# The first mixer's modulation pieces on TensorE: four strips of 32 columns in place of a share between TensorE and VectorE, and no subtractions on GpSimd in that phase

## The chip, the cores and the metric

The kernel runs on one core of one Trainium2 chip. The metric is the device time of one execution in microseconds (us); for a kernel it is the median of its runs. The core's engines have queues of their own and wait for each other by semaphores: TensorE (PE; its weight loads are listed apart as PEld), VectorE (DVE), ScalarE (ACT), GpSimd (POOL), and SyncE (SP), which here only starts DMA transfers. Each queue is worked off in its own fixed order.

## The reference, cut to what matters

Two layers of a trunk, on 256 tokens of 1024 numbers, everything in float32. A condition vector `c` steers each layer through six modulation vectors of 1024 numbers:

```python
c_act = jax.nn.silu(c)
for l in range(DEPTH):
    mod = c_act @ w_ada[l] + b_ada[l]
    sh_m, sc_m, g_m, sh_f, sc_f, g_f = [m[:, None, :] for m in jnp.split(mod, 6, -1)]
    h = rms_norm(x, norm_mix[l]) * (1.0 + sc_m) + sh_m
    proj = h @ w_in[l]
    ...
    y = (gate_a * y_a + gate_b * y_b) @ w_out[l]
    x = x + g_m * y
    h = rms_norm(x, norm_ffn[l]) * (1.0 + sc_f) + sh_f
    ...
    x = x + g_f * f
```

So nothing of the first projection `h @ w_in[0]` can be multiplied before the shift `sh_m` and the scale `sc_m` of layer 0 are known. They are 2048 of the 6144 columns of `c_act @ w_ada[0]`, a product of one row of 1024 numbers with a matrix of 8 MB. The layers' mixers (a gated delta rule and a sparse attention) and feed-forward parts (dense in layer 0, eight experts in layer 1) follow.

## The kernel before, in words

**Layout.** Activations lie transposed: 128 features on the partitions, 8 tiles of features (`k` = 0 to 7), 256 tokens along a row. A modulation vector must therefore end as columns, feature on partition; they stand in `modc`. The weights come from memory in pieces of 1 MB (512 columns by 4 feature tiles), one after the other on SP's queue, into slots that are used again when their readers are done.

**A modulation piece, `ada` (L248) and `flush` (L264).** A piece is 512 columns of `w_ada`, two transfers of four feature tiles each. Multiplying by `c_act` and adding over features is done in two ways. TensorE's part (L256): `cact[:, k]`, one column, is the stationary operand, and the 512 columns stream past it into row 0 of the bank `pada`. VectorE's part (L258, L260): each of the 128 partitions multiplies its 512 numbers by its own `cact` and adds them into `acc`, so the sum over partitions is still open. `NPE` says how many of the eight tiles TensorE takes: 4, 4, 0 and 2 for the pieces at columns 0, 1024, 512 and 1536. `flush` adds TensorE's row to row 0 of `acc` (L271), closes the sum over partitions and turns it into columns by four matmuls with a column of ones (L283), and adds the bias into `modc` (L285). `flush` of a piece is called after the next piece's products.

**The input of the mixer, `norm_mod` (L316 on).** For each feature tile VectorE scales `xT` into `hm0f` (L340), ScalarE adds the shift and rounds to float32r, giving `hm0h` (L341), and VectorE forms the rest that the rounding lost, `hm0l` (L344). It runs in two halves of four tiles: `part=0` needs the pieces 0 (shift) and 1024 (scale), `part=1` the pieces 512 and 1536.

**The weights of the projection, `split` (L218 on).** Each weight block is split in the same way: ScalarE rounds it (`wh`, `wnh`, L233), another engine subtracts to get the rest (`wl`, `wnl`, L235). Each product is then three matmuls: rounded by rounded, and the two cross terms (L239 to L241 in `chunk_b`, L370 to L372 in `chunk_t`). Which engine subtracts is `cur["lo"]`; in the phase in question it is set to GpSimd, later to VectorE.

**The phase.** TensorE transposes `x` (L125); pieces 0 and 1024; half 0 of the input; then the first halves of three projection blocks, begun while half 1 of the input is not there yet: 264 columns of `b` (`pn`), 512 columns of `k` and, after the pieces 512 and 1536, 512 columns of `q` (`pj`). Then half 1 of the input, and everything that needs all eight tiles. Beside this GpSimd computes angles for the position tables (`tables`, L390 on), which end in a sine on ScalarE (L417).

**Order.** Up to `manual.close()` PE, DVE and SP do their work in the order in which the code is written; ACT's and POOL's order is set by the scheduler's own model of times. After that the scheduler orders all engines but SP until the experts.

Of the kernel before, what the change touches and what calls it, by code (L numbers as in the profile page):

```python
# [9 lines left out]
F32 = mybir.dt.float32  # L10
F32R = mybir.dt.float32r
I32 = mybir.dt.int32
AF = mybir.ActivationFunctionType
OP = mybir.AluOpType
AX = mybir.AxisListType

P = 128
D = 1024
KT = 8
# [2 lines left out]
SPLM = 1  # L22
RAWM = 2
QTAG = (("pj", "dn", "ns"), ("dn", "ns", "pj"))
NPE = (4, 4, 0, 2)
S = 256
NT = 2
PIN = 5416
# [58 lines left out]
def trunk(ctx, tc, A, out, dbg=None, stop=None):  # L87
# [11 lines left out]
    cur = {}  # L99

    def bank(tag, name="ps"):
        if tag == "mi":
            seq["mi"] = seq.get("mi", -1) + 1
            tag = ("no", "pj", "pj")[seq["mi"] % 3]
        return cur["psum"].tile([P, 512], F32, tag=tag, name=name, bufs=cur["bufs"][tag])
# [8 lines left out]
    mm = nc.tensor.matmul  # L114
    V, SC, G = nc.vector, nc.scalar, nc.gpsimd
# [37 lines left out]
    ini = es0.enter_context(tc.tile_pool(name="init", bufs=1))  # L153
# [20 lines left out]
    cact = cst.tile([P, 8], F32, name="cact")  # L174
# [2 lines left out]
    V.tensor_scalar(cact, cact, 1.0, None, op0=OP.add)  # L177
    V.reciprocal(cact, cact)
    V.tensor_tensor(cact, cact, pt[:, 0:8], op=OP.mult)
    b_ada = cols[:, 0, 0:96]  # L180
    n_mix = cols[:, 0, 96:112]
    n_ffn = cols[:, 0, 112:128]
# [5 lines left out]
    acc = act.tile([P, NT, D], F32, tag="acc", name="acc")  # L188
# [14 lines left out]
    def load(src, k, n, name, per=0):  # L203

        per = per or min(k, 2048 // n // 4 * 4)
        rs = []
        for k0 in range(0, k, per):
            r = slot_raw(name)
            m = min(per, k - k0)
            r = r[:, :m * n].rearrange("p (k n) -> p k n", k=m)  # L210
            nc.sync.dma_start(r, src[:, k0:k0 + m])
            rs.append(r)
        return lambda k_, n_=None: rs[k_ // per][:, k_ % per] if n_ is None else rs[k_ // per][:, k_ % per:k_ % per + n_]
# [31 lines left out]

    pend = []

    def ada(l, o, tag="pj", npe=0, turn=False):  # L248


        w = load(A["w_ada"][l][:, o:o + 512].rearrange("(k p) n -> p k n", p=P), KT, 512, f"ada{l}_{o}")
        acc = cur["tmp"].tile([P, 512], F32, tag="adacc", name=f"adacc{l}_{o}", bufs=2)
        pa = bank(tag, "pada") if npe else None
        for k in range(KT):
            if k % 4 < npe // 2:
                mm(pa[0:1], cact[:, k:k + 1], w(k), start=k == 0, stop=k == KT - 5 + npe // 2)  # L256
            elif k == npe // 2:
                V.tensor_scalar(acc, w(k), cact[:, k:k + 1], None, op0=OP.mult)  # L258
            else:
                V.scalar_tensor_tensor(acc, w(k), cact[:, k:k + 1], acc, op0=OP.mult, op1=OP.add)  # L260
        flush()
        pend.append((l, o, acc, tag, pa, turn))

    def flush():  # L264
        if not pend:
            return
        l, o, acc, tag, pa, turn = pend.pop()
        if pa is None:
            pa = bank(tag, "pada")
        else:  # L270
            V.tensor_tensor(acc[0:1], acc[0:1], pa[0:1], op=OP.add)  # L271
        if turn:

            red = cst.tile([P, 16], F32, tag="red", name="red", bufs=2)
            for i in range(2):
                tt = cur["tmp"].tile([P, S], F32, tag="ht", name="adat", bufs=3)
                V.transpose(tt, acc[:, i * S:i * S + S])
                V.tensor_reduce(red[:, i * 8:i * 8 + 8], tt.rearrange("p (b r) -> p b r", r=32), axis=AX.X, op=OP.add)
            for q in range(4):
                mm(pa[q * 32:q * 32 + 32, 0:4], C["mod32"], red[:, q::4], start=True, stop=True)  # L280
        else:
            for j in range(4):
                mm(pa[:, j:j + 1], acc[:, j * P:(j + 1) * P], ones[:, 0:1], start=True, stop=True)  # L283
        j0 = o // P
        V.tensor_tensor(modc[l][:, j0:j0 + 4], pa[:, 0:4], b_ada[:, l * 48 + j0:l * 48 + j0 + 4], op=OP.add)  # L285
# [25 lines left out]
    def norm_scale(sums, name):  # L311

        return rsq(sums[:, 0:NT], 2, 1.0 / D, name + "r", None)
# [1197 lines left out]
    for t in range(NT):  # L1511
        for q in range(2):
            px = bank("dn", "px")
            for j in range(4):
                k = q * 4 + j
# [2 lines left out]
    ss = cst.tile([P, NT], F32, name="ss")  # L1518
    for t in range(NT):
        SC.activation(cur["tmp"].tile([P, D], F32, tag="sqx", name="sqx"), xtok[:, t], AF.Square, accum_out=ss[:, t:t + 1])  # L1520
    ada(0, 0, npe=NPE[0])
    rx = norm_scale(ss, "hm0")
    columns(0, r1)
    V.tensor_scalar(cols[:, 0, 96:128], cols[:, 0, 96:128], 1.5, None, op0=OP.mult)
    ada(0, 1024, npe=NPE[1])
    pb = norm_bc(rx)
    pbs = ini.tile([P, S], F32, name="pbs")
    SC.activation(pbs, pb[:, 0:S], AF.Copy)
# [4 lines left out]
    raw_k = win_half(0, 512, 512)  # L1533
    raw_q = win_half(0, 0, 512)
    hx = norm_mod(0, 0, "hm0", pbs, part=0)
    cur["lo"] = G
    begun[O_B] = [bank("ns", "pn") for _ in range(NT)]
    chunk_t(begun[O_B], raw_b, hx, 264, (0,))
    begun[512] = [chunk_b(raw_k, hx, j * P, tag="pj", ks=(0,)) for j in (0, 2)]
    ada(0, 512, "no", npe=NPE[2])  # L1540
    small(0)
    ada(0, 1536, "dn", npe=NPE[3])
    begun[0] = [chunk_b(raw_q, hx, j * P, tag="dn", ks=(0,)) for j in (0, 2)]
    small(1)
    tables()
# [70 lines left out]
```

## Time and profile before

| what | value |
|---|---|
| time, median of 3 runs | 1790.15 us (1789.74 to 1791.38) |
| profiled execution | 1790.63 us, of it span of the trace 1788.8 us |
| PE busy | 1715.6 us, 96% of the span |
| DVE busy | 1263.3 us, 71% |
| ACT busy | 934.4 us, 52% |
| POOL busy | 61.7 us, 3% |
| read from memory | 512.13 MB |

A row of the timeline gives the start and the length in us, the engine, the line in the kernel, the operation with the tile that it writes and those that it reads, its shape, and the number of instructions that were merged into it; in brackets stands how long the engine was idle before it and what ended that. A float32 matmul leaves two records on PE, so the four products of a piece are "x8". A "busy" time can hold stalls inside an instruction: the same shape on the same engine with a longer time is a sign of it.

### The profile page before, as it was taken

The page shows a single profiled execution, that of the slowest core. Times are in us where ns is not written, and L with a number is a line of the kernel's source. Part 1 is how long each engine was busy: PE and PEld are TensorE (multiplying, and loading weights), DVE is VectorE, ACT ScalarE, POOL GpSimd, SP SyncE. Part 2 cuts the span into 40 slices and gives each one's busy share as a digit, 9 for nine tenths or more (in the row PEclk, how much of TensorE's full clock was granted, in tenths as well). Part 3 has the DMA queues.
Part 4 walks back from the last instruction along what each step waited for, and adds up shares of the span by engine and source line. Part 5 has one row for each costly group of instructions (what it writes and reads, how often), then busy time and mean ns, then how long its engine had stood idle before and what let it go on. Part 6 is the DMA issues. An engine that isn't in the chain of part 4 may idle for free.

```text
span 1788.8 us, 29436 instructions
## 1 busy us (share of the span) xinstructions
PE 1715.6 (96%) x11324; PEld 1373.2 (77%) x11324; DVE 1263.3 (71%) x2138; ACT 934.4 (52%) x1370; POOL 61.7 (3%) x114
## 2 busy tenths in 40 slices
PE   6988999899999999999999999999999999999997
PEld 4885988899999897888888635788884467888732
DVE  6758956799996767836698614988983078999711
ACT  3655453444444575554587504777772067777500
POOL 4300000100000100000200000000000000000000
PEclk8887998999999899999999999999999999999999
DMA  9553545699984344226779899999999999999997
GB/s 331 164 174 114 179 130 189 211 353 325 328 289 154 118 141 134 72 95 212 283 288 381 323 407 407 409 403 409 374 357 367 403 409 406 406 395 364 344 391 279
DMA packets 206362, 515.17 MB, mean 288 GB/s; under 512 B 18862, under 2 KB 58358, under 8 KB 206214
## 3 DMA queue, kind: packets, MB, share of 16 engines
q1 hardware_dynamic: 196806, 509.25, 77.1%
q10 hardware_dynamic: 9312, 3.90, 0.8%
q8 instruction: 91, 1.49, 0.3%
q14 instruction: 57, 0.47, 0.1%
q0 software_dynamic: 96, 0.07, 0.0%
HBM read 512.13 MB, written 1.05 MB: 287 GB/s over the span
## 4 chain that ended last, share of the span: by engine, by line
PE 91%; DVE 5%; ACT 2%; DMA 1%; issue 1%; POOL 0%; ACTq 0%; DVEq 0%
PE ph L1221 21%; PE py L1252 11%; PE pj L239 8%; PE ph L1284 8%; PE pj L241 8%; PE pj L240 8%; PE py L1311 4%; PE py L241 2%; PE py L239 1%; PE py L240 1%; PE pSs L894 1%; PE pob L914 1%; PE pg L1154 1%; PE put L125 1%; PE pn L370 1%; PE pn L371 1%
## 5 line engine op out<-in xcount | busy, mean ns | idle before, releaser
L235 DVE TENSOR_TENSOR wml<-m,wmh 128x1024 fp32r<-128x1024 f32 (+1 forms) x300 | 310.8, 1076 | 35.8 <-ACT wmh L233 32.3
L233 ACT ACTIVATE wmh<-m 128x1024 fp32r<-128x1024 f32 (+1 forms) x302 | 276.5, 945 | 63.4 <-PE ph L1221 35.4
L1221 PE MATMUL ph<-wml,gh 128*128 128x512 f32 x560 | 181.8, 397 | 2.0 <-DVE wml L235 2.0
L1221 PE MATMUL ph<-wmh,gl 128*128 128x512 f32 x560 | 181.8, 394 | 0.0
L1221 PE MATMUL ph<-wmh,gh 128*128 128x512 f32 x560 | 181.7, 394 | 0.0
L233 ACT ACTIVATE w2h<-m 128x1024 fp32r<-128x1024 f32 x130 | 134.6, 1056 | 41.7 <-PE py L1252 27.8
L235 DVE TENSOR_TENSOR w2l<-m,w2h 128x1024 fp32r<-128x1024 f32 x130 | 152.4, 1218 | 4.8 <-ACT w2h L233 4.3
L1252 PE MATMUL py<-w2h,uu 128*128 128x512 f32 x560 | 152.9, 394 | 0.0
L1284 PE MATMUL ph<-m,gs 128*64 128x512 f32 (+1 forms) x720 | 139.7, 537 | 0.0
L1221 PEld LDWEIGHTS ph<-wml,gh 128*128 128x128 f32 x560 | 103.8, 188 | 32.1 <-DVE wml L235 7.3
L239 PE MATMUL pj<-hf0h,wh 128*128 128x256 f32 x448 | 127.0, 285 | 1.2 <-ACT hf0h L341 1.2
L240 PE MATMUL pj<-hf0l,wh 128*128 128x256 f32 x448 | 126.4, 283 | 0.0
L241 PE MATMUL pj<-hf0h,wl 128*128 128x256 f32 x448 | 125.6, 283 | 0.0
L1221 PEld LDWEIGHTS ph<-wmh,gh 128*128 128x128 f32 x560 | 105.0, 188 | 25.6 <-ACT wmh L233 1.6
L1252 PEld LDWEIGHTS py<-w2h,uu 128*128 128x128 f32 x560 | 105.1, 188 | 24.5
L1221 PEld LDWEIGHTS ph<-wmh,gl 128*128 128x128 f32 x560 | 105.1, 188 | 24.3
L260 DVE SCALAR_TENSOR_TENSOR adacc<-ada,cact,adacc 128x512 f32<-128x512 f32 x158 | 116.8, 756 | 2.4 <-DMA ada<-in_w_ada_dram 1.4
L1284 PEld LDWEIGHTS ph<-m,gs 128*64 128x64 f32 x720 | 51.3, 137 | 81.9 <-issue 73.7
L233 ACT ACTIVATE wh<-w 128x1024 fp32r<-128x1024 f32 x56 | 59.5, 1062 | 93.1 <-PE pj L240 62.0
L1294 DVE TENSOR_TENSOR u<-u,ph 128x512 f32<-128x512 f32 (+1 forms) x12 | 7.4, 620 | 136.2 <-PE ph L1284 136.2
L233 ACT ACTIVATE wh<-win 128x1024 fp32r<-128x1024 f32 x64 | 67.2, 1055 | 62.3 <-PE pj L240 45.4
L235 DVE TENSOR_TENSOR wl<-win,wh 128x1024 fp32r<-128x1024 f32 x60 | 73.3, 1224 | 29.4 <-ACT wh L233 29.2
(643 smaller groups left out, 3965.8 us busy)
## 6 DMA issues: line engine op xcount, KB each, us to landing
m<-in_w_moe_dram SPq DMA_DIRECT2D x313, 1024.0 KB, 12.4
ada<-in_w_ada_dram SPq DMA_DIRECT2D x48, 1024.0 KB, 8.0
w<-in_w_dense_dram SPq DMA_DIRECT2D x42, 1024.0 KB, 7.4
win<-in_w_in_dram SPq DMA_DIRECT2D x34, 1024.0 KB, 5.1
xT<-in_w_moe_dram SPq DMA_DIRECT2D x23, 1024.0 KB, 12.1
wout<-in_w_out_dram SPq DMA_DIRECT2D x8, 1024.0 KB, 5.3
win<-in_w_in_dram SPq DMA_DIRECT2D x8, 536.0 KB, 3.8
win<-in_w_in_dram SPq DMA_DIRECT2D x8, 528.0 KB, 3.6
```

What stands on the lines that cost most here:

```text
L125: return nc.tensor.transpose(out_, in_, ident[:k, :k])
L233: SC.activation(hi, src, AF.Copy)
L235: cur["last"] = eng.tensor_tensor(lo, src, hi.bitcast(F32), op=OP.subtract).ins
L239: mm(o, w[0], x[0], start=start, stop=False, skip_group_check=True)
L240: mm(o, w[0], x[1], start=False, stop=False, skip_group_check=True)
L241: mm(o, w[1], x[0], start=False, stop=stop, skip_group_check=True)
L260: V.scalar_tensor_tensor(acc, w(k), cact[:, k:k + 1], acc, op0=OP.mult, op1=OP.add)
L370: mm(o, x[0][:, kt, s], hi[:, k], start=kt == 0, stop=False)
L1221: mm(p_, s_[:, k], d_[:, i * 512:i * 512 + 512], start=k == 0 and d_ is hi and s_ is gh, stop=k == KT - 1 and d_ is lo)
L1252: mm(p_, s_[:, j], d_[:, n * 512:n * 512 + 512], start=q + j == 0 and d_ is hi and s_ is uh, stop=q == 3 and j == nb - 1 and d_ is lo)
L1284: mm(p_[i * 64:i * 64 + 64, 0:h], self.g[:, k], raw[:, i * h:i * h + h], start=k == 0, stop=k == KT - 1, skip_group_check=True)
L1311: mm(self.py[n * 64:n * 64 + 64], self.u[q][:, b, i * 64:i * 64 + 64], raw[:, n * 512:n * 512 + 512], start=q + j == 0, stop=q == 3 and j ...
```

## The change

`cactz` is a copy of `cact` in which each column is followed by 31 columns of zeros. With it a product of one feature tile fills a strip of 32 columns of the stationary side and 32 rows of the bank: tiles `k` = 0 to 3 go to the strips 0, 32, 64 and 96, tiles 4 to 7 are added on the same strips. For the four pieces of layer 0's mixer input all eight tiles go this way; VectorE's products and the addition of the row (L271) go, and ScalarE copies the whole bank to `acc` instead. The other pieces stay on VectorE as before, now without a share for TensorE. The line that gave the subtractions of the phase to GpSimd is gone, so VectorE does them. Lines behind the change move by 1 or 2 (L235 is now L237, L285 is L286).

```diff
-NPE = (4, 4, 0, 2)
...
+    cactz = ini.tile([P, KT, 32], F32, name="cactz")
+    G.memset(cactz, 0.0)
+    V.tensor_copy(cactz[:, :, 0], cact)
...
-    def ada(l, o, tag="pj", npe=0, turn=False):
+    def ada(l, o, tag="pj", tiled=False, turn=False):
...
-        pa = bank(tag, "pada") if npe else None
-        for k in range(KT):
-            if k % 4 < npe // 2:
-                mm(pa[0:1], cact[:, k:k + 1], w(k), start=k == 0, stop=k == KT - 5 + npe // 2)
-            elif k == npe // 2:
-                V.tensor_scalar(acc, w(k), cact[:, k:k + 1], None, op0=OP.mult)
-            else:
+        if tiled:
+            pa = bank(tag, "pada")
+            for k in range(KT):
+                q = k % 4 * 32
+                mm(pa[q:q + 32], cactz[:, k], w(k), start=k < 4, stop=k >= KT - 4, skip_group_check=True)
+            SC.activation(acc, pa, AF.Copy)
+        else:
+            V.tensor_scalar(acc, w(0), cact[:, 0:1], None, op0=OP.mult)
+            for k in range(1, KT):
                 V.scalar_tensor_tensor(acc, w(k), cact[:, k:k + 1], acc, op0=OP.mult, op1=OP.add)
         flush()
...
-        if pa is None:
-            pa = bank(tag, "pada")
-        else:
-            V.tensor_tensor(acc[0:1], acc[0:1], pa[0:1], op=OP.add)
+        pa = bank(tag, "pada")
...
-    ada(0, 0, npe=NPE[0])
+    ada(0, 0, tiled=True)
...
-    ada(0, 1024, npe=NPE[1])
+    ada(0, 1024, tiled=True)
...
-    cur["lo"] = G
...
-    ada(0, 512, "no", npe=NPE[2])
+    ada(0, 512, "no", tiled=True)
     small(0)
-    ada(0, 1536, "dn", npe=NPE[3])
+    ada(0, 1536, "dn", tiled=True)
```

How the instructions stand, on VectorE between the two halves of the input (`adacc_512` and `adacc_1536` are the sums of the pieces 512 and 1536, `win_2048`, `win_512` and `win_0` the blocks of `b`, `k` and `q`). Before:

```order
L344 SCALAR_TENSOR_TENSOR hm0l<-hm0f,modc_106,hm0h 128x256 x2
L258 TENSOR_SCALAR adacc_512_318<-ada_512_314,cact 128x512
L260 SCALAR_TENSOR_TENSOR adacc_512_318<-ada_512_314,cact,adacc_512_318 128x512 x3
L260 SCALAR_TENSOR_TENSOR adacc_512_318<-ada_512_316,cact,adacc_512_318 128x512 x4
L258 TENSOR_SCALAR adacc_1536_337<-ada_1536_333,cact 128x512
L260 SCALAR_TENSOR_TENSOR adacc_1536_337<-ada_1536_333,cact,adacc_1536_337 128x512 x2
L260 SCALAR_TENSOR_TENSOR adacc_1536_337<-ada_1536_335,cact,adacc_1536_337 128x512 x3
L285 TENSOR_TENSOR modc_106<-pada,cols 128x4
L271 TENSOR_TENSOR adacc_1536_337<-adacc_1536_337,pada 1x512
L285 TENSOR_TENSOR modc_106<-pada,cols 128x4
L334 SCALAR_TENSOR_TENSOR hm0am<-modc_106,cols 128x4
```

The same place after the change:

```order
L345 SCALAR_TENSOR_TENSOR hm0l<-hm0f,modc_109,hm0h 128x256 x2
L237 TENSOR_TENSOR wnl<-win_2048_205,wnh 128x1056
L237 TENSOR_TENSOR wl<-win_512_207,wh 128x1024 x2
L286 TENSOR_TENSOR modc_109<-pada,cols 128x4
L237 TENSOR_TENSOR wl<-win_0_209,wh 128x1024 x2
L286 TENSOR_TENSOR modc_109<-pada,cols 128x4
L335 SCALAR_TENSOR_TENSOR hm0am<-modc_109,cols 128x4
```

The products have left, and five subtractions stand in their place: three of them behind the last `hm0l` of half 0, and the two of `q` behind the addition of piece 512 into `modc`.

On ScalarE, from the rounding of the block `b` to the sine (`pbs` is the tokens' scale, `cs` the sine's tile). Before:

```order
L233 ACTIVATE wnh<-win_2048_200 128x1056
L233 ACTIVATE wh<-win_512_202 128x1024 x2
L1528 ACTIVATE pbs<-pb 128x256
L341 ACTIVATE hm0h<-hm0f,modc_106 128x256 x4
L233 ACTIVATE wh<-win_0_204 128x1024 x2
L233 ACTIVATE wnh<-win_2048_479 128x1056
L233 ACTIVATE wh<-win_512_581 128x1024 x2
L417 ACT_TABLE_LOAD
L417 ACTIVATE cs<-cs 128x192
L1509 ACTIVATE cols<-pcol 128x128
L341 ACTIVATE hm0h<-hm0f,modc_106 128x256 x2
```

After:

```order
L235 ACTIVATE wnh<-win_2048_205 128x1056
L1529 ACTIVATE pbs<-pb 128x256
L342 ACTIVATE hm0h<-hm0f,modc_109 128x256 x2
L235 ACTIVATE wh<-win_512_207 128x1024 x2
L342 ACTIVATE hm0h<-hm0f,modc_109 128x256 x2
L235 ACTIVATE wh<-win_0_209 128x1024 x2
L260 ACTIVATE adacc_512_323<-pada 128x512
L418 ACT_TABLE_LOAD
L418 ACTIVATE cs<-cs 128x192
L260 ACTIVATE adacc_1536_344<-pada 128x512
L235 ACTIVATE wnh<-win_2048_487 128x1056
L235 ACTIVATE wh<-win_512_589 128x1024 x2
```

The two roundings of `k` now stand between the second and the third `hm0h` of half 0, and the sine with its table stands ahead of the next blocks' roundings and no longer right ahead of `hm0h` of half 1; what follows the last row shown is two copies to `cols` and then four `hm0h`.

## Rows read from the trace of the kernel before

**Rows 1.** The page's row of 40 slices for PE (busy share of each slice of 44.7 us in tenths) and the first line of its part on the chain that ended last (shares of the span by engine).

```profile
PE   6988999899999999999999999999999999999997
PE 91%; DVE 5%; ACT 2%; DMA 1%; issue 1%; POOL 0%; ACTq 0%; DVEq 0%
```

**Rows 2.** Busy times by stretch: bounds in us, length, busy time and number of instructions of each engine, granted TensorE clock as a share of full speed, DMA share, GB/s.

```profile
24.00:28.40 4.40, 0.00 (x0) 0.00 (x0) 4.17 (x3) 0.58 (x3) 3.59 (x2) 0.50 1.04 386
28.40:34.00 5.60, 5.53 (x25) 5.51 (x26) 5.26 (x10) 1.43 (x4) 2.23 (x5) 0.50 1.03 315
...
55.70:61.00 5.30, 5.28 (x24) 5.29 (x25) 2.97 (x8) 0.94 (x4) 5.30 (x16) 0.50 0.97 275
```

**Rows 3.** Timeline of PE and PEld, 12 to 24 us: pieces 0 and 1024 (L256) with a transpose for `cols` between them, their turning into columns (L283), and the spreading of the tokens' scale (`pb`).

```profile
12.04 4.41 PE L256 MATMUL pada<-ada,cact 128*1 128x512 f32 x8
16.38 0.33 PE L125 MATMUL pcol<-ct,r 128*128 128x128 f32 x1
16.64 3.59 PE L256 MATMUL pada<-ada,cact 128*1 128x512 f32 x8
17.93 0.08 PEld L256 LDWEIGHTS pada<-ada,cact 128*1 128x1 f32 x1 [0.34 <-DMA ada<-in_w_ada_dram]
20.64 1.05 PE L283 MATMUL pada<-ct,adacc 128*128 128x1 f32 x8 [0.40 <-DVE adacc L271]
21.55 0.41 PE L125 MATMUL pb<-ct,hm0ry 128*128 128x128 f32 x2
22.52 1.05 PE L283 MATMUL pada<-ct,adacc 128*128 128x1 f32 x8 [0.56 <-DVE adacc L271]
```

**Rows 4.** Timeline of PE, 28 to 56 us: the first product with a subtracted block of `b`, the first of `k`, piece 1536, the turning of piece 512, the third product of `q`, the turning of piece 1536, two transposes for `cols`, and the first product of the second half.

```profile
28.85 0.42 PE L371 MATMUL pn<-wnl,hm0h 128*128 128x264 f32 x1
...
33.99 0.38 PE L239 MATMUL pj<-hm0h,wh 128*128 128x256 f32 x1
...
39.84 1.88 PE L256 MATMUL pada<-ada,cact 128*1 128x512 f32 x4
41.65 1.05 PE L283 MATMUL pada<-ct,adacc 128*128 128x1 f32 x8
...
42.89 0.28 PE L241 MATMUL pj<-hm0h,wl 128*128 128x256 f32 x1
...
48.30 0.95 PE L283 MATMUL pada<-ct,adacc 128*128 128x1 f32 x8
49.11 0.31 PE L125 MATMUL pcol<-ct,r 128*128 128x128 f32 x1
51.39 0.47 PE L125 MATMUL pcol<-ct,r 128*128 128x128 f32 x1 [1.97 <-ACT cols L1509]
...
55.72 0.59 PE L371 MATMUL pn<-wnl,hm0h 128*128 128x264 f32 x1 [2.27 <-DVE wnl L235]
```

**Rows 5.** Timeline of DVE: from the second `modc` to half 0 of the input, one product of piece 1536, and the same steps in half 1 up to the subtraction for the second half of `b`.

```profile
23.61 0.16 DVE L285 TENSOR_TENSOR modc<-pada,cols 128x4 f32<-128x4 f32 x1 [1.14 <-PE pada L283]
23.81 1.50 DVE L334 SCALAR_TENSOR_TENSOR hm0am<-modc,cols 128x4 f32<-128x4 f32 x1
25.42 2.85 DVE L340 SCALAR_TENSOR_TENSOR hm0f<-xT,hm0am,pbs 128x256 f32<-128x256 f32 x2
...
39.14 2.58 DVE L258 TENSOR_SCALAR adacc<-ada,cact 128x512 f32<-128x512 f32 x1
...
49.28 0.16 DVE L285 TENSOR_TENSOR modc<-pada,cols 128x4 f32<-128x4 f32 x1 [2.89 <-PE pada L283]
49.48 0.16 DVE L334 SCALAR_TENSOR_TENSOR hm0am<-modc,cols 128x4 f32<-128x4 f32 x1
49.68 0.88 DVE L340 SCALAR_TENSOR_TENSOR hm0f<-xT,hm0am,pbs 128x256 f32<-128x256 f32 x2
51.76 0.48 DVE L344 SCALAR_TENSOR_TENSOR hm0l<-hm0f,modc,hm0h 128x256 fp32r<-128x256 f32 x1 [1.21 <-ACT hm0h L341]
...
54.41 1.25 DVE L235 TENSOR_TENSOR wnl<-win,wnh 128x1056 fp32r<-128x1056 f32 x1
```

**Rows 6.** Timeline of POOL: subtractions of `k` and of `q`.

```profile
22.95 4.64 POOL L235 TENSOR_TENSOR wl<-win,wh 128x1024 fp32r<-128x1024 f32 x2 [0.22 <-ACT wh L233]
...
38.73 2.71 POOL L235 TENSOR_TENSOR wl<-win,wh 128x1024 fp32r<-128x1024 f32 x1
```

**Rows 7.** Timeline of ACT: a copy of a whole bank, a copy to `cols`, the roundings of `k`, the table for the sine, and the first two `hm0h` of half 1.

```profile
12.15 0.60 ACT L1517 ACTIVATE xT<-px 128x512 f32<-128x512 f32 x1 [0.23 <-PE px L125]
16.75 0.28 ACT L1509 ACTIVATE cols<-pcol 128x128 f32<-128x128 f32 x1 [4.00 <-PE pcol L125]
...
21.81 2.00 ACT L233 ACTIVATE wh<-win 128x1024 fp32r<-128x1024 f32 x2 [1.63 <-DMA win<-in_w_in_dram]
...
49.51 1.28 ACT L417 ACT_TABLE_LOAD   x1
...
51.23 0.90 ACT L341 ACTIVATE hm0h<-hm0f,modc 128x256 fp32r<-128x256 f32 x2
```

**Rows 8.** Timeline of PE in the experts, a stretch of products whose stationary side is 64 columns wide and alternates between two strips of the bank (rows 0 to 63 and 64 to 127), float32, 512 columns streaming, as in L256.

```profile
1059.68 4.89 PE L1284 MATMUL ph<-m,gs 128*64 128x512 f32 x22
```

**Rows 9.** Busy times by stretch in the first mixer (columns as in rows 2).

```profile
60.00:260.00 200.00, 183.78 (x1691) 164.56 (x1690) 149.00 (x413) 111.42 (x248) 7.40 (x25) 0.89 0.46 154
140.00:150.00 10.00, 6.13 (x25) 4.33 (x26) 10.00 (x25) 7.37 (x19) 0.00 (x0) 0.84 0.39 135
```

More of the change, by code (lines that the diff above doesn't have):

```diff
@@ L246, in trunk @@
     pend = []
-    def ada(l, o, tag="pj", npe=0, turn=False):
+    def ada(l, o, tag="pj", tiled=False, turn=False):
         w = load(A["w_ada"][l][:, o:o + 512].rearrange("(k p) n -> p k n", p=P), KT, 512, f"ada{l}_{o}")
         acc = cur["tmp"].tile([P, 512], F32, tag="adacc", name=f"adacc{l}_{o}", bufs=2)
-        pa = bank(tag, "pada") if npe else None
-        for k in range(KT):
-            if k % 4 < npe // 2:
-                mm(pa[0:1], cact[:, k:k + 1], w(k), start=k == 0, stop=k == KT - 5 + npe // 2)
-            elif k == npe // 2:
-                V.tensor_scalar(acc, w(k), cact[:, k:k + 1], None, op0=OP.mult)
-            else:
+        if tiled:
[7 more added lines that the diff above has]
+            for k in range(1, KT):
                 V.scalar_tensor_tensor(acc, w(k), cact[:, k:k + 1], acc, op0=OP.mult, op1=OP.add)
         flush()
-        pend.append((l, o, acc, tag, pa, turn))
+        pend.append((l, o, acc, tag, turn))
     def flush():
@@ L266, in flush @@
             return
-        l, o, acc, tag, pa, turn = pend.pop()
-        if pa is None:
-            pa = bank(tag, "pada")
-        else:
-            V.tensor_tensor(acc[0:1], acc[0:1], pa[0:1], op=OP.add)
+        l, o, acc, tag, turn = pend.pop()
+        pa = bank(tag, "pada")
         if turn:
```

## The prediction

> **What bounds the kernel now.** I read the page first. PE holds 91% of the chain that ended last, and its busy row is at 8 or 9 in nearly every slice but the first [rows 1]: a change in the first 60 us is worth what it moves the moment from which PE runs through. Then the timeline of each engine in that stretch. The reader is to see three places there where something other than PE's products ends last. First, the first input half: PE finishes piece 1024, waits for DVE's addition twice, and the second `modc` comes at 23.61 [rows 3, 5]; then DVE takes 1.50 us for an `hm0am` that takes 0.16 at 49.48, and 2.85 for two `hm0f` that take 0.88 at 49.68. Both stretches lie on POOL's subtractions of `k` (22.95 to 27.59), as the 2.58 us of the product at 39.14 lies on that of `q` at 38.73 [rows 5, 6]. PE has nothing from 24.0 to 28.4, and its granted clock is 0.50, the lower level (1.2 of 2.4 GHz), there and until 34.0 [rows 2]. Second, from 28.85 to 48.30 PE is the bound itself: `b`, `k`, piece 1536, `q` without a gap worth the name [rows 4]. Third, the second half: `modc` at 49.28, then DVE waits 1.21 us for ACT, which is loading the sine's table in front of `hm0h`, and PE goes on at 55.72, again at 0.50 until 61 [rows 2, 4, 5, 7].
>
> **The price of a strip.** The trace of before has no product in four strips. It has them in two: 22 records in 4.89 us, 0.222 each [rows 8], where the same stream in one place took 3.59 for eight, 0.449 each [rows 3]. Two strips therefore run side by side at full speed. I take the same for four, 0.111 a record, so 1.78 us for a piece of sixteen records. The ends are 0.111 and 0.449 (no overlap); 0.222 is the nearest row if only two fit. The Trainium skill ("TensorE: Matmul & The Clock Gate", the section on packing small matmuls, its measured speedups) speaks against the full factor: four row strips gave 3.07 and three column strips 2.38. By that a piece would take 7.18 / 3.07 = 2.34 us, an estimate from that page, and the sum below would end 1.4 us later (half a piece on the first path, two on the second); two strips here lost nothing, and no run here shows more.
>
> **First half.** TensorE now has all eight tiles of a piece. Piece 0 is done well before piece 1024 has landed and its copy (0.60 on ACT, [rows 7]) is hidden in that wait. The last half of piece 1024 is there at 17.93 at the latest [rows 3]; eight records make 0.89, so PE is done at 18.82 where it was done at 20.23. Now nothing stands between: turning of piece 0 (0.91 from start to start), `pb` 0.41, turning of piece 1024 at 20.14; the copy of its bank (18.8 + 0.2 + 0.60) is ready before that. `modc` comes 1.09 behind (22.52 to 23.61), at 21.23 instead of 23.61. With POOL silent, `hm0f` follows 0.40 later (as 49.28 to 49.68), at 21.63, and `hm0h` half a us behind it, at 22.13.
>
> That 2.4 us is not kept. ACT's order now has the two roundings of `k` (2.00) between the second and the third `hm0h` [rows 7]: the pair takes 0.90, so the third starts at 22.13 + 0.90 + 2.00 = 25.03, its `hm0l` 0.53 later (51.23 to 51.76), the last one 0.45 behind, and `wnl` of `b`, which POOL had long done in the old order, now stands in DVE's queue behind that: start 26.4, 1.25 long [rows 5], and PE's second product of `b` at 27.73 (0.06 behind, as 55.66 to 55.72). Before it was 28.85 [rows 4]. Gain: 1.12 us. The subtractions of `k` follow on DVE in 2.5 us while PE needs 5.14 for `b`, so they are hidden. PE's gap stays, so I keep the lower clock as it was.
>
> **Middle.** From there before's own distances: 5.14 to the first product of `k` (32.87), 5.85 to the end of `k` (38.72). There stood 1.81 us of piece 1536; now both pieces 512 and 1536 stand there, 32 records, 3.55 us: 42.27. Their data is there by then: VectorE was at piece 1536 from 39.14, PE at tiles of both its transfers from 39.84, neither with a wait [rows 4, 5]. Then the turning of 512. Here is the added wait: DVE's addition into `modc` waits for it (0.98 behind its start, as 48.30 to 49.28: 43.25), and behind it in DVE's queue stand the two subtractions of `q`. The first ends at 43.45 + 1.25 = 44.70; PE, which has two products of `q` that need only the rounded block, stands until 44.76 at the third, which before came at 42.89. From it 5.41 to the turning of 1536 (42.89 to 48.30): 50.17, so half 1 is 1.87 us late at this point: 1.12 gained, 1.74 for the added records, 1.25 for the stall.
>
> **Second half.** `modc` is at 51.15. Before, `hm0h` waited for the sine. That has moved between the copies of 512 and 1536, where ACT has time, since POOL's angles are no longer interleaved with subtractions of 2.4 us. What is late next is `cols`: ACT's order has both copies ahead of `hm0h`. The transpose starts 0.81 behind the turning (48.30 to 49.11), 50.98; the copy 0.37 later (16.38 to 16.75) and 0.28 long [rows 3, 7]; the second transpose uses the same bank [rows 4] and so starts at 51.68, its copy ends at 52.33. `hm0h` at 52.33, `hm0l` at 52.86 instead of 51.76. The rest is before's: PE goes on at 55.72 + 1.10 = 56.82.
>
> **At nothing** I cost `cactz` (a memset on POOL and a small copy on DVE before 9 us, with the first product at 12.04 as cover; about 0.2 us if that were gone), the copies of the pieces 0, 512 and 1536 on ACT (each has more than a us before its turning), and DVE's products of 512 and 1536 that leave: they stood beside PE's stream, which ran through after 28.85. Those of 0 and 1024 and the additions to the row are in the first half's gain.
>
> **The sum.** The first 57 us become 1.1 us longer. Behind them PE runs on, so I carry it to the end: 1790.63 + 1.10 = 1791.7 for an execution like the profiled one, which was 0.48 above the median; on the median of the runs 1791.2. The scheduler has ordered the first mixer anew, on ACT, DVE and PE; that order I can't price from rows. PE is idle 16.2 us of the 200 there [rows 9], which bounds a gain; I take nothing for it, with some 3 us to either side.
>
> **Rivals.**
> *The strips don't overlap by four* (the other side). Decides at piece 1024, and again between `k` and `q`. By twos (0.222): 0.89 more in the first half and 3.55 in the middle, 1.1 + 4.4 = 5.5, so 1795.7. Not at all (0.449): pieces 0 and 1024 end at 12.04 + 8.0 + 7.2 = 27.2 instead of 18.8, and the middle takes 14.4 instead of 3.55: 1.1 + 8.4 + 10.8 = 20.3, so 1810.5. For it: no row with four. Against: two lost nothing.
> *A better order in the first mixer.* A third of PE's 16.2 idle us would be 5.4: 1790.15 + 1.1 - 5.4 = 1785.9. For: DVE is fully busy at 140 to 150 while PE is at 6.1 of 10 [rows 9], so DVE's order decides there. Against: its work in that stretch is the same as before.
> *A worse one.* DVE's chain of small operations for the delta rule's keys (`rqk0`) now stands behind the products of piece 2048, and its end is what the delta rule's products wait for. The same third the other way: 1796.7.
>
> **Chances.** My forecast, nearly no change, 0.58; no overlap by four 0.14 (0.08 by twos, 0.06 none); a better order 0.15; a worse one 0.13. What can be told from no change is 0.2%, 3.6 us. So faster 0.15, within 0.58, slower 0.14 + 0.13 = 0.27. The range from 1785.8 (the better order) to 1797.0 (the worse order and the strips by twos) leaves out the rest of either order and the strips that don't overlap, not quite 0.2.
>
> **What would show it.** Sixteen records of a piece in about 1.8 us, against 3.6 or 7.2; `hm0am` at 0.16 in both halves and `modc` near 21.2; the third `hm0h` 2 us behind the second; `pn` with `wnl` near 27.7; PE idle about 1.2 us at the third product of `q`, with DVE's `wl` as its releaser; PE going on near 56.8. Wrong would be a PE stream that starts on `b` 3 us or more before 28.85, a clock that stays up in the gap, or a first mixer whose end (before: the stretch to 260) moves by more than the start.

## The result, and the profile after

The changed kernel takes 1800.8 us (median of 4 runs, 1799.45 to 1804.03) where the kernel before takes 1790.77 (4 runs beside it): ratio 1.0067 (1.0052 to 1.0082), 10 us slower. The ratios in this text are those on record, taken over the fast runs; they are not the quotients of two medians (here 1.0056). Forecast were 1791.2 us and a range to 1797.0. A second set of runs of it gave 1.0071 (after_again, below).

The page first: its row for PE, with the row of the granted clock under it, in slices of 45 us. The first three slices are as in [rows 1]; the fourth (135 to 180 us) has gone from 8 to 7 and the seventh (270 to 315) from 9 to 8, both in the first mixer, and the clock of the fourth is 0.6. The last row is the clock before, where the fourth slice has 0.7.

```profile
PE   6987998899999999999999999999999999999997
PEclk8996899999999899899999999999999999999999
PEclk8887998999999899999999999999999999999999
```

The timeline of PE in the start phase, from both pieces to the first product of half 1 with a subtracted block (to compare with [rows 3, 4]):

```profile
11.75 1.93 PE L259 MATMUL pada<-ada,cactz 128*32 128x512 f32 x16
14.83 1.06 PE L259 MATMUL pada<-ada,cactz 128*32 128x512 f32 x8 [0.90 <-DMA ada<-in_w_ada_dram]
17.55 1.06 PE L259 MATMUL pada<-ada,cactz 128*32 128x512 f32 x8 [1.66 <-DMA ada<-in_w_ada_dram]
...
27.03 0.59 PE L372 MATMUL pn<-wnl,hm0h 128*128 128x264 f32 x1 [4.19 <-DVE wnl L237]
...
37.95 3.64 PE L259 MATMUL pada<-ada,cactz 128*32 128x512 f32 x32
...
43.97 0.39 PE L243 MATMUL pj<-hm0h,wl 128*128 128x256 f32 x1 [1.05 <-DVE wl L237]
...
56.00 0.59 PE L372 MATMUL pn<-wnl,hm0h 128*128 128x264 f32 x1 [2.62 <-DVE wnl L237]
```

The same steps on DVE (with [rows 5]):

```profile
20.69 0.16 DVE L286 TENSOR_TENSOR modc<-pada,cols 128x4 f32<-128x4 f32 x1 [0.90 <-PE pada L284]
20.89 0.16 DVE L335 SCALAR_TENSOR_TENSOR hm0am<-modc,cols 128x4 f32<-128x4 f32 x1
...
24.93 0.88 DVE L345 SCALAR_TENSOR_TENSOR hm0l<-hm0f,modc,hm0h 128x256 fp32r<-128x256 f32 x2 [1.02 <-ACT hm0h L342]
25.73 1.25 DVE L237 TENSOR_TENSOR wnl<-win,wnh 128x1056 fp32r<-128x1056 f32 x1
...
42.62 0.16 DVE L286 TENSOR_TENSOR modc<-pada,cols 128x4 f32<-128x4 f32 x1 [13.37 <-PE pada L284]
42.70 2.36 DVE L237 TENSOR_TENSOR wl<-win,wh 128x1024 fp32r<-128x1024 f32 x2
```

On ACT, the roundings of `k` and the third and fourth `hm0h` of half 0 behind them (with [rows 7]):

```profile
22.51 1.99 ACT L235 ACTIVATE wh<-win 128x1024 fp32r<-128x1024 f32 x2
24.40 0.89 ACT L342 ACTIVATE hm0h<-hm0f,modc 128x256 fp32r<-128x256 f32 x2
```

And the stretches (with [rows 2, 9]), first after:

```profile
55.70:61.00 5.30, 5.00 (x28) 5.00 (x29) 3.33 (x10) 1.45 (x6) 5.30 (x15) 0.65 0.94 264
60.00:260.00 200.00, 179.83 (x1631) 157.76 (x1631) 147.00 (x414) 110.02 (x249) 8.54 (x26) 0.88 0.43 143
130.00:140.00 10.00, 4.16 (x36) 3.95 (x34) 8.48 (x31) 3.06 (x3) 0.00 (x0) 0.90 0.81 296
140.00:150.00 10.00, 6.18 (x15) 4.25 (x16) 9.98 (x40) 5.11 (x16) 0.00 (x0) 0.50 0.62 212
150.00:160.00 10.00, 10.00 (x33) 6.16 (x32) 7.97 (x25) 2.10 (x7) 0.00 (x0) 0.50 0.00 0
```

Then before, for the two stretches around the one in [rows 9]:

```profile
130.00:140.00 10.00, 10.00 (x81) 9.63 (x81) 8.91 (x26) 3.70 (x8) 0.00 (x0) 1.00 0.97 329
150.00:160.00 10.00, 7.65 (x26) 4.84 (x24) 9.94 (x39) 3.05 (x9) 0.00 (x0) 0.50 0.46 168
```

Up to 60 us nothing is lost. The strips overlap by four, and although PE goes on with half 1 at 56.00 (55.72 before), its clock rises sooner (0.65 in the row from 55.70, 0.50 before), so that the same instructions of PE stand 0.81 us *earlier* than before from 60 to 95 us. That is one execution. The same start phase stands in ten profiles, this one and those of nine kernels below that have the whole change. In three of them PE is 0.78 to 0.81 us early, in seven 0.04 to 1.73 us late (median of the ten: 0.2 late). In the three the granted clock was 1.00 until 21.8 us; in the seven it fell between 17.4 and 19.9 us, and the second `modc` comes at 21.15 to 23.36 instead of 20.69 to 20.80. The loss begins at 130 us: PE has 4.16 of 10 us there (before: 10.00), and its clock then is 0.50 for 20 us (before: 0.84, then 0.50). What stands on that place on DVE, first before and then after: the key chain of the delta rule from `rqk0a` over the first `cx` and `kb` to its first product `L`.

```profile
113.82 0.19 DVE L137 TENSOR_SCALAR rqk0a<-pq 128x32 f32<-128x32 f32 x1 [1.77 <-PE pq L648]
...
135.76 0.41 DVE L689 COPY cx<-cb 128x512 f32<-128x512 f32 x1
...
139.02 0.69 DVE L695 TENSOR_TENSOR kb<-qk,pc 128x512 f32<-128x512 f32 x1 [1.09 <-PE pc L125]
...
147.05 1.27 DVE L725 TENSOR_TENSOR L<-pS,eb 128x512 f32<-128x512 f32 x2
```

```profile
122.39 0.19 DVE L136 TENSOR_SCALAR rqk0a<-pq 128x32 f32<-128x32 f32 x1 [0.31 <-PE pq L649]
...
142.71 0.40 DVE L690 COPY cx<-cb 128x512 f32<-128x512 f32 x1
...
146.27 0.67 DVE L696 TENSOR_TENSOR kb<-qk,pc 128x512 f32<-128x512 f32 x1
...
153.45 0.68 DVE L726 TENSOR_TENSOR L<-pS,eb 128x512 f32<-128x512 f32 x1
```

PE waits for it: its first product with `cx` comes after 9.10 us of idle time (the row names `rr`, the small instruction right behind `cx` in DVE's queue), where before it came without a gap. Again before, then after:

```profile
138.39 0.60 PE L125 MATMUL pc<-ct,cx 128*128 128x128 f32 x4
```

```profile
143.26 1.09 PE L124 MATMUL pc<-ct,cx 128*128 128x128 f32 x4 [9.10 <-DVE rr L834]
```

### The profile page after: what moved, and what is told of

Its sections match the earlier page's. It is cut to its first block, busy times and chain, and to the rows that moved or that the text cites. A ratio compares the mean times of both kernels' runs of the same rounds, so it can differ in the third digit from the quotient of the medians.

```text
span 1798.5 us, 29500 instructions
## 1 busy us (share of the span) xinstructions
PE 1716.9 (95%) x11368; PEld 1372.3 (76%) x11368; DVE 1244.9 (69%) x2119; ACT 936.0 (52%) x1374; POOL 48.6 (3%) x110
## 3 DMA queue, kind: packets, MB, share of 16 engines
HBM read 512.13 MB, written 1.05 MB: 285 GB/s over the span
## 5 line engine op out<-in xcount | busy, mean ns | idle before, releaser
L237 DVE TENSOR_TENSOR wml<-m,wmh 128x1024 fp32r<-128x1024 f32 (+1 forms) x300 | 311.1, 1077 | 35.4 <-ACT wmh L235 32.5
L235 ACT ACTIVATE wmh<-m 128x1024 fp32r<-128x1024 f32 (+1 forms) x302 | 276.4, 945 | 64.8 <-PE ph L1222 36.2
L235 ACT ACTIVATE w2h<-m 128x1024 fp32r<-128x1024 f32 x130 | 134.6, 1056 | 41.6 <-PE py L1253 27.8
L237 DVE TENSOR_TENSOR w2l<-m,w2h 128x1024 fp32r<-128x1024 f32 x130 | 152.5, 1219 | 4.8 <-ACT w2h L235 4.4
L235 ACT ACTIVATE wh<-w 128x1024 fp32r<-128x1024 f32 x56 | 59.5, 1062 | 94.6 <-PE pj L242 60.4
L237 DVE TENSOR_TENSOR wl<-win,wh 128x1024 fp32r<-128x1024 f32 x64 | 77.9, 1222 | 40.2 <-ACT wh L235 39.8
L264 DVE SCALAR_TENSOR_TENSOR adacc<-ada,cact,adacc 128x512 f32<-128x512 f32 x140 | 101.7, 742 | 0.3
L235 ACT ACTIVATE wh<-win 128x1024 fp32r<-128x1024 f32 x64 | 67.2, 1055 | 65.4 <-PE pj L242 43.9
```

The source lines that it names most:

```text
L235: SC.activation(hi, src, AF.Copy)
L237: cur["last"] = eng.tensor_tensor(lo, src, hi.bitcast(F32), op=OP.subtract).ins
```

## The experiments

**Theory.** The start phase does what was predicted; the loss is in the order that the scheduler made of everything behind it. **Rival.** The phase itself costs it later: through its strips, VectorE's subtractions, its transfers or the clock. Behind `manual.close()` both kernels have the same 8104 instructions with the same operands; only their order differs (474 of 1232 places on DVE, 1984 of 5963 on PE, 144 of 684 on ACT, 5 of 145 on SP). So the order can be exchanged: it is stored as a list and laid on as edges that set only the sequence in an engine's queue. Shortened (the list is stored packed):

```diff
+def hold(tc, nc, first):
+    traced = nc.cur_bb.bb.instructions[first:]
+    for e, order in HELD.items():
+        mine = [traced[k] for k in order]
+        for a, b in zip(mine, mine[1:]):
+            tc.add_manual_dep(b, a.name, DependencyInfo(NoSync, DATA), reason="hold")
```

*after_order_of_before*: the changed kernel, held in before's order. 

> The changed start phase, and from its end to the end of layer 1's mixer every engine's instructions held in the order in which the kernel before has them. If the order alone costs the 10 us: 1790.0 us (ratio 0.9995, within 0.998 to 1.001), the instructions at 60 to 95 us stand 0.8 us earlier than before and so do those at 145 and at 340 us. If the loss comes from what the phase itself does (its products on four strips, the subtractions on VectorE, its transfers, the clock): about 1800 us (ratio 1.005 or more), with a shift at 145 us of several us.

Measured: 0.9996 (0.9984 to 1.0008), -0.78 us at 60 to 80 us.

*before_order_of_after*: the other way round. 

> The start phase of before, with the rest up to the end of layer 1's mixer held in the order of the changed kernel. If the order costs it: 1801 us (ratio 1.0057, within 1.004 to 1.008), with rqk0a on VectorE at about 123 us and the first product L at about 154 us. If the phase costs it: 1790.8 us (ratio 1.000).

Measured: 1.0041 (1.0027 to 1.0056), `rqk0a` at 123.04 and `L` at 152.68. The order alone makes a kernel slower that has nothing of the change, and without it the change costs nothing. The rival falls as a cause by itself. But the same order costs more behind the changed phase (1.0067, and 1.0071 in the second set) than behind the old one; the intervals of 1.0041 and of 1.0071 do not touch, though the two were timed on different chips, each beside before. By these numbers some 5 us arise only where the order and the changed phase meet, and no run shows how.

*strips_only* and *subs_only*: the two halves of the change, the first with `cur["lo"] = G` put back behind `norm_mod(..., part=0)`, the second the kernel before without that line; both in before's order.

```diff
     hx = norm_mod(0, 0, "hm0", pbs, part=0)
+    cur["lo"] = G
     begun[O_B] = [bank("ns", "pn") for _ in range(NT)]
```

> Strips for the four pieces, the subtractions of the phase back on GpSimd, order held as before. The first half then waits for wnl of 4.64 us on GpSimd as before, so the strips gain little there; the middle has 32 records of four strips (3.6 us) for four of 0.47. At 70 us I expect -0.3 us against before (between -1.5 and +1.5), and 1790.5 us in all. If the two halves of the change are additive and the strips carry the loss, it is +2 us or more.

> The pieces multiplied as before, only the subtractions of the phase moved from GpSimd to VectorE, order held as before. VectorE then has the products of the pieces and the subtractions of 1.25 to 2.35 us each in one queue: at 70 us I expect +1.5 us against before (between -0.5 and +4), and 1792.3 us in all. If VectorE has room in the phase, it is below 0.

Measured: 0.9994 (0.9981 to 1.0007) and 1.0012 (0.9996 to 1.0028). At 60 to 80 us they stand at -0.78 and +1.03 us, the same for all instructions there. (In the expectation of strips_only the 4.64 us are the two subtractions of `k`; that of `b`, `wnl`, took 2.46.) No gain of the subtractions is seen, and the strips alone stand where the full change stands in its earliest profiles. But each is one profile, the strips of strips_gpsimd and strips_late_pieces stand at -0.65 and +0.36, and the full change at -0.8 to +1.7: the halves are not told apart to a microsecond. In strips_only PE goes on at 54.93, in the full change's first profile at 56.00, and they end up at the same place because the clock rises later in strips_only:

```profile
54.93 0.59 PE L372 MATMUL pn<-wnl,hm0h 128*128 128x264 f32 x1 [2.28 <-DVE wnl L237]
```

```profile
55.70:61.00 5.30, 5.30 (x27) 5.30 (x26) 2.56 (x9) 1.29 (x4) 5.30 (x19) 0.51 1.05 298
```

*strips_gpsimd*: strips_only with nothing held. 

> The strips with the subtractions of the phase back on GpSimd, nothing held: the scheduler by itself comes to the order of before in all engines. It is strips_only without the list, so the same 0.9994 (0.998 to 1.001) and a shift of -0.8 us at 60 to 80 us are expected; a ratio over 1.003 would say that holding an order by itself makes a kernel faster, and the runs with held orders would tell less.

Measured: 0.9986 (0.9975 to 0.9997). Left to the scheduler, the strips keep before's order in all 8104 places, and so does the moved subtraction alone. Only the two together tip it. Holding an order is not what made the held kernels faster.

*after_again* and *first_mixer_as_before*: the changed kernel once more, beside the next three on one chip, and the changed kernel with before's order in the first mixer alone. 

> The changed kernel as it is, beside the three others on one chip. Its loss was 1.0067 (1.0052 to 1.0082) where it was first timed; the two runs that held an order gave 0.9996 for the phase and 1.0041 for the order, together 1.0037. I expect 1.005, and rqk0a on VectorE at 122.4 us, the first product L at 153.5 us, as in the first trace.

> The changed kernel with its own order, but the first mixer in the order of before (TensorE, ScalarE, VectorE); the dense part and layer 1's mixer in the order of the changed kernel. If the first mixer's order is the loss, some 6 of the 10 us come back: ratio 1.002 (1.000 to 1.004), and the instructions at 340 us stand at or ahead of before. If the orders of the dense part and of layer 1's mixer carry it, the ratio stays at 1.005 or more.

Measured: 1.0071 (1.0058 to 1.0083), with `rqk0a` at 123.83 and `L` at 155.56 in a profile whose start phase ends 1 us later than in the first, and 1.0014 (1.0001 to 1.0026). Most of the loss is the first mixer's order. The rest comes behind it: from 330 us to the experts the instructions of after, after_again and key_chain_moved lose another 4.2 to 4.5 us, those of first_mixer_as_before 3.4, of after_order_of_before 0.9.

**Which of its differences?** First the one that the rival in the prediction named.

*key_chain_moved*: the changed order, in which only the squares, their products `pq` and DVE's 17 instructions from `rqk0a` to `cx` stand where before has them. 

> The changed kernel with its own order, and in it one thing moved to where before has it: the chain of the key norms (the last squares sq on ScalarE, their products pq on TensorE, on VectorE the 17 instructions rqk0a to bk, cb, acc and the first cx). If this chain is the cause in the first mixer: rqk0a at 113 to 114 us, the first kb at 139 to 140, the first product L at 147.5 (153.45 in the changed kernel), and 5 to 7 us of the time come back: ratio 1.002 (1.000 to 1.004). If it is the order of the other work there (the norms rn0 and rc0, npk, npq, kvc ahead of the delta rule), L comes at 152 us or later and the ratio stays at 1.005.

Measured: 1.0064 (1.0051 to 1.0076). `cx` comes at 132.34, 10 us sooner, but `kb` at 146.10 and `L` at 151.97. PE's one wait has become two, for the decay factor and for `kb`:

```profile
141.97 1.22 PE L713 MATMUL pd<-gs,masks 128*128 128x512 f32 x2 [5.38 <-ACT eb L709]
146.92 1.19 PE L724 MATMUL pS<-kb,qk 64*128 64x256 f32 x2 [2.88 <-DVE kb L696]
```

*key_chain_first*: a higher priority for these lines. 

> The changed kernel, its order made by the scheduler, with the squares, products and norms of the keys (lines 642 to 657) given a higher priority (300 instructions earlier), so that VectorE has bk and the first cx ahead of most of the products of piece 2048. If the delta rule's chain sets the end of this stretch, the first L comes at 141 to 146 us and the time falls below both kernels: 1783 us, ratio 0.997 (0.993 to 1.000). If the order of the mixer is worth its noise alone, it lies anywhere between 0.998 and 1.006.

```diff
+        with tc.high_priority(300):
             pq = bank("dn", "pq")
             ...
             V.tensor_scalar(rq, rqk[:, :, 0], 0.125, None, op0=OP.mult)
```

Measured: 1.0062 (1.0046 to 1.0078). `L` comes at 130.61, the delta rule runs 15 us ahead until 210 us, and at 330 us PE is 10.4 us behind: the sparse branch is late now (its last product `pob` starts at 292.1, before at 271.4). The expectation, a gain, missed.

*norms_behind_L*: edges that put DVE's instructions of lines 617 to 632 (`nsa`) behind the second `L` (`put`).

```diff
+                    for ins in nsa:
+                        if ins.engine == put.ins.engine:
+                            tc.add_manual_dep(ins, put.ins.name, DependencyInfo(NoSync, DATA))
```

> The changed kernel, its order made by the scheduler, with one rule added: on VectorE the instructions that apply the norms of the sparse branch (lines 617 to 632: npk, npq, qs, qr) stand behind the delta rule's second product L. Moving the key chain alone had put bk 17 us earlier and the first L only 1.5 us, since kb and L still stood behind these instructions. If they are what holds the delta rule, kb follows its cx within 3 us (144 to 146 us, 146.3 before), the first L comes at 148 to 150.5 us (153.45 in the changed kernel), and 2 to 4 us of the loss come back: ratio 1.0045 (1.003 to 1.006). If the first mixer's loss lies later (after 180 us), the ratio stays at 1.0065 although L comes earlier.

Measured: 1.0081 (1.0067 to 1.0095). `kb` does follow its `cx` within 1.7 us, but `L` comes no sooner (155.12, in a profile whose start phase ends 2.5 us later than in the first of the changed kernel), and both ratios expected missed.

*pin_pq*, *pin_sq_pq*: one edge on TensorE, and the same with one on ScalarE (the second line); the names stand for the places that the code gives by number.

```diff
+        tc.add_manual_dep(pn_product, last_pq.name, DependencyInfo(NoSync, DATA))
+        tc.add_manual_dep(wnh_rounding, last_sq.name, DependencyInfo(NoSync, DATA))
```

> The changed kernel with one edge more: on TensorE the first product pn behind the twelfth square product pq stays behind the last pq (in the changed kernel 48 of these products went ahead of it). The scheduler then has the key chain early and the delta rule's L ahead of the sparse branch's npk on VectorE, both, as in before, without the order of before elsewhere. If these two together are what the first mixer lost: rqk0a at 114 us, L at 145 to 149 us and ahead of the first npk product, ratio 1.000 to 1.003. If the loss needs the whole order of before, it stays at 1.005 or more.

> The same edge and one more on ScalarE (the rounding wnh behind the last square). The scheduler now has the key chain early too, but npk ahead of L on VectorE, as in the changed kernel. If it takes both, as above: L at 151 us or later, ratio 1.004 to 1.008. If the early key chain is enough, or if any early chain is: 1.000 to 1.003.

Measured: 1.0133 (1.0115 to 1.0151) and 1.0014 (1.0003 to 1.0025), the reverse of what I expected. In pin_pq `L` is ahead of `npk`, but `rqk0a` comes at 120.01 and `L` at 151.03, not at 114 and 145 to 149: this kernel is the slowest of all. pin_sq_pq, with `npk` (146.21) ahead of `L` (150.44), has lost next to nothing. When the first `L` comes does not tell the loss.

*vector_held*: DVE alone in before's order. 

> The changed kernel with VectorE alone held in the order of before; TensorE and ScalarE are the scheduler's, which comes within 213 of 5963 and 23 of 684 places of before. If VectorE's order is the carrier, the ratio is that of the fully held one: 0.9996 (0.998 to 1.001). If the places that still differ on TensorE matter, 1.002 or more.

Measured: 1.0048 (1.0032 to 1.0065). With the same order on DVE the few places that differ on PE make DVE itself wait: `rqk0a` at 123.53 after 10.37 us without work, released by PE's `pq`. VectorE's order alone does not carry it; TensorE's alone and ScalarE's alone were not tried.

**What the orders have in common.** For each profile I took the shift of PE's instructions against the trace of before (median over the same instructions) at 66 to 80 and at 322 to 340 us; the difference is what the first mixer cost. Over the same stretch (95 to 330 us, the bounds moved by these shifts) I added, in slices of 5 us, PE's idle time and the clock not granted (the share not granted times the length: 10 us at 0.50 count 5).

| profile | mixer, us | PE idle | clock not granted |
|---|---|---|---|
| before | 0 | 16.3 | 25.9 |
| subs_only | -1.1 | 15.8 | 25.4 |
| strips_gpsimd | -3.2 | 14.8 | 24.3 |
| strips_only | -5.3 | 15.3 | 20.8 |
| first_mixer_as_before | -6.7 | 14.9 | 20.2 |
| after_order_of_before | -6.8 | 15.0 | 20.1 |
| pin_sq_pq | -3.9 | 18.6 | 18.3 |
| vector_held | +2.0 | 17.9 | 25.4 |
| before_order_of_after | +1.4 | 20.9 | 24.3 |
| after, after_again | +6.1, +6.0 | 21.7, 22.1 | 27.0, 27.0 |
| key_chain_moved | +5.5 | 20.2 | 27.0 |
| key_chain_first | +9.9 | 17.6 | 33.8 |
| norms_behind_L | +13.0 | 18.8 | 38.9 |
| pin_pq | +20.5 | 16.8 | 49.4 |

The two columns together account for the first: against before, their sum differs from the mixer's cost by at most 3.5 us in any row of the table. This is bookkeeping: a stretch is PE's idle time and its busy time, and the same products take longer where less clock is granted. It tells where the cost lies, not which difference of the order made it. (The clock column counts idle stretches too, though nothing is lost by the clock there.) The first six rows have before's order; they spread over 7 us, by the clock above all (each is one profile, and a profiled execution lies up to 3.4 us off its kernel's median). Against their means (15.4 and 22.8) the changed kernel's two profiles have 6.5 us more of idle time and 4.2 us more of clock not granted; against the one trace of before it is 5.4 to 5.8 us and 1.1. And the slowest three have only 1.4 to 3.4 us more idle time than those means, but 11 to 27 us more of clock not granted. In pin_pq, 240 to 270 us:

```profile
240.00:250.00 10.00, 10.00 (x239) 7.92 (x232) 2.42 (x6) 3.58 (x9) 0.00 (x0) 0.50 0.03 10
250.00:260.00 10.00, 9.73 (x127) 6.82 (x124) 3.21 (x12) 6.27 (x16) 0.00 (x0) 0.50 0.01 2
260.00:270.00 10.00, 10.00 (x57) 7.04 (x55) 6.60 (x13) 2.29 (x6) 0.00 (x0) 0.50 0.27 83
```

PE is busy for 29.7 of these 30 us, at the lower clock. Its costliest groups there (busy us, mean ns):

```profile
L895 PE MATMUL pSs<-kT,qT 64*128 64x512 f32 x8 | 8.3, 1138 | 0.0
L915 PE MATMUL pob<-npk,pT 128*128 128x64 f32 x32 | 7.9, 428 | 0.0
L124 PE MATMUL ppt<-ct,pr 128*128 128x128 f32 x16 | 4.6, 428 | 0.3 <-ACT pr L905 0.3
```

The same products in after_order_of_before, 215 to 245 us, where the clock is 1.00:

```profile
L242 PE MATMUL pj<-hm0l,wh 128*128 128x256 f32 x27 | 7.9, 291 | 0.0
L241 PE MATMUL pj<-hm0h,wh 128*128 128x256 f32 x27 | 7.8, 289 | 0.0
L243 PE MATMUL pj<-hm0h,wl 128*128 128x256 f32 x26 | 7.7, 294 | 0.0
L895 PE MATMUL pSs<-kT,qT 64*128 64x512 f32 x10 | 5.6, 641 | 0.0
L915 PE MATMUL pob<-npk,pT 128*128 128x64 f32 x32 | 4.4, 281 | 0.0
```

There the weights' products `pj` stand between the small ones. In pin_pq they had been used up earlier, and the attention's and the inversion's products were left alone. No run changed that alone, so what kept the clock low there is not shown.

**A kernel that beats both.** Between 119 and 149 us DVE has 16 products of the pieces 2048 and 2560 before (0.73 us most of them), four of them at 140 to 150 us, where PE is idle for 3.9 of 10 us [rows 9]. *strips_late_pieces* gives them to the strips too. The diff shows one of its three places: `cactz` also moves to a pool that lives longer, and `cur["lo"] = G` stands as in strips_gpsimd.

```diff
-                        ada(0, 2048 + 512 * j)
+                        ada(0, 2048 + 512 * j, tiled=i == 0)
```

> The strips, subtractions on GpSimd, and the pieces 2048 and 2560 of the first mixer also multiplied by TensorE on four strips (32 records, 3.6 to 7 us by the clock granted there) in place of 16 products of 0.73 us (11.7 us) on VectorE, which is busy for all of 138 to 160 us while TensorE idles. The order is the scheduler's. If VectorE's queue sets this stretch, the first L comes at 138 to 143 us and the time is 1784 us, ratio 0.997 (0.994 to 0.999); if the other branch ends last, as when the key chain was put first, nothing is gained: 1.000 to 1.006.

Measured: 1781.7 us, 0.9958 (0.9944 to 0.9972), 8 us below before. The first `L` comes at 135.70, 11 us sooner, and PE is busy for 29.2 of the 30 us:

```profile
130.00:140.00 10.00, 10.00 (x66) 8.48 (x65) 8.54 (x34) 6.84 (x20) 0.00 (x0) 1.00 0.66 211
140.00:150.00 10.00, 10.00 (x62) 7.60 (x63) 8.97 (x30) 1.23 (x4) 0.00 (x0) 1.00 0.00 0
150.00:160.00 10.00, 9.18 (x54) 6.47 (x52) 9.46 (x26) 4.43 (x12) 0.00 (x0) 1.00 0.00 0
```

Its idle time from 95 to 330 us is 8.9 us and its clock not granted 15.8, the least of all. Here the bookkeeping of the table doesn't close: the two fall by 17.5 us against before, the first mixer by 6.7. PE has 32 records more to do (30 of them took 5.54 us), and the rest is not accounted for. Beside it strips_gpsimd took 1786.81 us (0.9986), so the late pieces and the order that came with them are worth some 5 of the 8 us; which of the two, no run tells.

## Why the prediction was wrong, point by point

**The price of a strip: right.** 1.93 us for sixteen records, 3.64 for 32, so 0.121 and 0.114 each (0.111 taken). The Trainium skill ("TensorE: Matmul & The Clock Gate", the section on packing small matmuls) has 3.07 for four row strips and 2.38 for three column strips. The estimate from its 3.07, 2.34 us a piece, was too long: four column strips gave 0.449 / 0.114 = 3.9 here in a running stream, and the measurement decides.

**First half: right in kind, gain too small for this execution.** `modc` came at 20.69 (21.23), the third `hm0h` at 24.40 (25.03), behind the roundings of `k` as drawn, and PE's product with `wnl` at 27.03: 1.82 gained instead of 1.12. `hm0am` took 0.16 with POOL silent, as taken. Over the ten profiles of this phase that product comes at 27.03 to 29.70, in the median at 27.76, where the forecast had 27.73.

**Middle: right.** The stall at the third product of `q` came as drawn: 1.05 us released by `wl`, at 43.97 (44.76).

**Second half: the distance right, its end missed.** PE went on 0.28 late instead of 1.1, since the first half had gained more. Then the clock rose earlier, which I had kept as it was; that turned +0.28 into -0.81. Over the ten profiles PE goes on at 56.00 to 58.56, in the median at 56.89 (forecast: 56.82).

**The sum: here is the step that failed.** "I take nothing for it, with some 3 us to either side", on the scheduler's new order in the first mixer. It cost some 10 us there in the median (1.0071 against 1.0014 with before's order in it), and another 3 to 4 behind it, which I had not looked at. "Behind them PE runs on, so I carry it to the end" failed with it: PE stood 9.10 us at 134 to 143 us and then ran at the lower clock. Of the three signs of being wrong that the prediction names, the third came, a first mixer that moves by more than the start (+6.1 against -0.8 us).

**The rival "a worse one"** had the right place and side. Its price was a third of PE's idle time, 5.4 us, about half of what the order cost. That the idle time from 95 to 330 us grew by just 5.4 (16.3 to 21.7) is chance; in the rival's own stretch of 60 to 260 us it grew by 4.0 (16.2 to 20.2). Not in it were the clock not granted (4.2 us over the mean of before's order) and the cost behind the first mixer. Its mechanism was read rightly from the order as the first wait, and yet moving that chain back gave back little: behind it the next wait stood ready. At 0.13 the rival was held for too unlikely: that the scheduler had ordered three engines anew was known, and no row said that the old order was average.

**"The strips don't overlap"** is excluded by the rows. **"A better order"** did not come: none of the other orders tried with the full change was faster than before's own (0.9996). strips_late_pieces is faster, with other work on PE and DVE as well as another order.

What stays open is which of the order's differences in the first mixer decides. The runs show that neither of the two named (the key chain, the sparse branch's norms ahead of `L`) gives the loss back alone, that the cost lies in idle time and clock, and that this order cost more behind the changed phase than behind the old one; they don't show a rule by which a good order could be told in advance.

## What to carry to other kernels

Where a scheduler orders by modelled times, a change of a us in one phase can order everything behind it anew, and here that cost some ten times what the change moved: compare the order first, and time the change once more with the old order laid on, before it is judged. A new order is priced by PE's idle time and by the clock that is not granted, and in the slowest three kernels here the second was the larger. The half of a change that shows no gain by itself (here the subtractions) is worth leaving out: the strips alone kept the old order and lost nothing. And a microsecond read from one profile wants a second profile: the same start phase ended 0.8 us early in one execution and 1.7 us late in another.

## What the runs showed of the hardware that was not expected

Four column strips of float32 products ran nearly four at a time, 0.114 us a record against 0.449 in one place, at a granted clock of 1.00 both times. TensorE was busy for 29.7 of 30 us in pin_pq and stayed at the lower clock (0.50, 1.2 of 2.4 GHz) all the while: `pob` took 428 ns there and 281 in after_order_of_before at 1.00, `pSs` 1138 and 641. A full busy row is no sign of a full clock. And a stretch that starts 1.07 us later can end at the same place: PE went on at 56.00 and at 54.93 in two profiles, with the clock back at 1.00 from 59.4 and from 60.9 us, and they stood at -0.81 and -0.78 us from 60 us on.
